# Weight stream of a 256-token model kernel: 1 MB slots and transfers become 512 KB ones, with the ends of the expert layers re-ordered

## The chip, the cores and the metric

The kernel runs on one core of a Trainium2 chip. The metric is the device time of one execution in microseconds (us), lower is better. Three executions of the kernel before took 1793.07, 1799.25 and 1799.32 us, a median of 1799.25. A further execution was profiled.

## The reference, cut to what matters

Everything is float32, 256 tokens of width 1024. A first block of two layers (a convolution and recurrence mixer, an mLSTM mixer, each with a SwiGLU feed-forward of width 2816) is followed by a second block of two layers, and each of these ends in a mixture of experts. The change touches how all weights reach the core, and the code of the mixture:

```
h = modulate(rms_norm(x, g_norm2), shift2, scale2)           # x is 256 x 1024
group  = argmax(h @ w_rg + b_rg)                             # 4 groups
expert = top-2 of the 8 experts of that group (h @ w_re + b_re)
gate   = softmax(group logits)[group] * softmax(top-2 logits)
y = sum over the two experts: gate * (silu(h @ w_gate[e]) * (h @ w_up[e])) @ w_down[e]
x = x + g2 * y
out = rms_norm(x, g_final)                                   # after the second of these layers
```

There are 32 experts of 1024 x 512, 1024 x 512 and 512 x 1024, 6 MB each, and every expert's weights are read in full in both layers: 384 MB of the kernel's 597 MB.

## The kernel before, in words

Weights stream from HBM through slots of 128 x 2048 floats (WT = 2048, 1 MB, rows of 8 KB per partition), all loaded on SyncE's queue (SP). `slot` (L364) hands them out in rotation. The dense weights come through `raw_w` (L389): one 1 MB transfer holds two operands of 128 x 1024, and `split` (L396) divides an operand into a high and a low part on ScalarE (L419) and VectorE (L420). The expert weights come through `load_expert` (L1560, the transfer at L1566): four transfers a matrix and pair of experts, twelve to a pair. `prefetch` fills all free slots ahead of the expert layer, about 20 of them. After that a load waits until TensorE is done with the slot, and it also waits for the landing of the load eight before it, since the framework gives the queue's transfers eight semaphores in turn.

An expert layer (`phase_moe`, L1584) starts with `route` (L1400): transposes of x, router logits, a chain of small VectorE operations that ends in `pos` (the place of every token in its expert's 64 slots) and `W` (its weight). Four matmuls that write an unused bank stand in the middle (NWR, L1432), and the operations for W have a low priority in the order of the queues. Then come 16 pairs of experts, in a fixed order on TensorE (`in_order`). `gather` (L1622) runs for two pairs at a time: eight selection tiles on VectorE (L1626) and four quarters of matmuls, each followed by two evictions into XT (L1637 on ScalarE, L1639 on VectorE). A pair (L1658) is the gate and the up product, silu and a multiply (L1663, L1664), the scatter of the pair before, transposes (L1672, L1681), the down product in two halves of 512 columns, and the split of its result (L1691, L427, L428). In the products the two experts stand side by side in the array, and the trace holds two records to each matmul of the code. `bcast_cols` (L1110) spreads g2 over the partitions with eight small products; it stands in pair 0, between the up product and the transposes.

After pair 5 (PROV) a branch (`overflow`, L1509 to L1558) handles experts with over 64 tokens. It isn't taken here, but its body issues transfers on SP. At the end of a layer `add_x` (L649) adds each token tile to x in two halves and forms the mean square, and after the second layer `final` (L1720) multiplies by the gain and stores four quarters on SP.

Of the kernel before, what the change touches and what calls it, by code (L numbers as in the profile page):

```python
# [16 lines left out]
S = 256  # L17
# [5 lines left out]
WT = 2048  # L23
# [21 lines left out]
NWR = 4  # L45
# [94 lines left out]
def host_layout(inp):  # L140
# [58 lines left out]
    st = np.stack(st).reshape(-1, 2, 128, 1024).transpose(0, 2, 1, 3).reshape(-1, 128, WT)  # L199
    out["wst"] = np.ascontiguousarray(st)  # L200

    a = g["w_ada_2"].reshape(2, 1024, 24, 2, 128).transpose(0, 2, 4, 3, 1)
    out["wada"] = np.ascontiguousarray(a).reshape(48, 128, WT)
# [55 lines left out]
    for n, k in (("w_gate_2", "wg"), ("w_up_2", "wu")):  # L259
        a = g[n].reshape(2, NEXP, 2, 4, 128, 512).transpose(0, 1, 2, 4, 3, 5)  # L260
        out[k] = np.ascontiguousarray(a).reshape(2, NEXP, 2, 128, WT)
    a = g["w_down_2"].reshape(2, NEXP, 4, 128, 2, 512).transpose(0, 1, 4, 3, 2, 5)
    out["wd"] = np.ascontiguousarray(a).reshape(2, NEXP, 2, 128, WT)
# [4 lines left out]
class K:  # L268
    def __init__(self, ctx, first, tc, A, out):
        self.ctx, self.tc, self.A, self.out = ctx, tc, A, out  # L270
        nc = self.nc = tc.nc
        self.slots, self.held, self.sps = [], [], []
        self.n_pool = 0
        self.const = ctx.enter_context(tc.tile_pool(name="const", bufs=1))
        self.sm = ctx.enter_context(tc.tile_pool(name="sm", bufs=4))
        self.taps = {}

        self.spare = ctx.enter_context(tc.tile_pool(name="spare", bufs=SPB))
# [64 lines left out]
    def ring(self, es, n, side=None):  # L343

        self.n_pool += 1
        pool = es.enter_context(self.tc.tile_pool(name=f"ring{self.n_pool}", bufs=n, **({"side": side} if side else {})))
        self.slots = [pool] * n + self.slots
        es.callback(lambda: setattr(self, "slots", [p for p in self.slots if p is not pool]))
# [40 lines left out]
    def raw_w(self):  # L389
        i = self.n_w  # L390
        self.n_w += 1
        if i % 2 == 0:
            self.cur_w = self.slot()
            self.last_w = self.nc.sync.dma_start(self.cur_w, self.A["wst"][i // 2])
        return self.cur_w[:, (i % 2) * 1024:(i % 2) * 1024 + 1024]

    def split(self, w):
# [3 lines left out]
        if sp is self.spare:  # L401
            hl = sp.tile([128, WT], F32R, name="w")
            hi, lo = hl[:, 0:n], hl[:, n:2 * n]
        else:
            hi = sp.tile([128, n], F32R, name="hi")
            lo = sp.tile([128, n], F32R, name="lo")
# [703 lines left out]
def bcast_cols(self, col, dst):  # L1110

    for h in range(2):
        ps = self.ps.tile([128, 512], F32, name="ps")
# [263 lines left out]
def moe_setup(self, l, p):  # L1377
# [12 lines left out]
    wrG = self.kvp.tile([128, 2, D], F32, name="cb")[:, 0].rearrange("p (k e) -> p k e", k=8)  # L1390
# [9 lines left out]
def route(self, raw, tmp, keep):  # L1400
# [15 lines left out]
    for t in range(2):  # L1416
        for h in range(2):
# [4 lines left out]
            if t == 0:  # L1422
                nc.scalar.activation(raw[:, t, 512 * h:512 * h + 512], ps, AF.Copy)
            else:
                nc.vector.tensor_copy(raw[:, t, 512 * h:512 * h + 512], ps)
        pl = self.pa.tile([128, 512], F32, name="pa")
        for k in range(8):
            self.mm(pl[:, 0:RN], raw[:, t, 128 * k:128 * k + 128], wrG[:, k, 0:RN], start=(k == 0), stop=(k == 7))
# [48 lines left out]
    with self.background():  # L1477
# [14 lines left out]
    return rs, pos, W  # L1492
# [16 lines left out]
def overflow(self, l, p, rs, pos, W, fl, acc, w, hid, hT, XT, g2):  # L1509
# [4 lines left out]
    with tc.If(flag):  # L1514
# [4 lines left out]
        for t in range(2):  # L1519
            nc.sync.dma_start(wd[t], wv[:, t])  # L1520
        for t in range(2):
# [6 lines left out]
            with tc.For_i(0, NEXP, 1) as e:  # L1528
                wc = p.tile([128, 1], F32, name="wc", bufs=2)
                nc.sync.dma_start(wc, wd[t, :, ds(e, 1)])  # L1530
                gu = []
                for nm in ("wg", "wu"):
                    ps = self.gu.tile([128, 512], F32, name="gu")
                    for q in range(4):
                        nc.sync.dma_start(w, self.A[nm][l, ds(e, 1), q // 2, :, 1024 * (q % 2):1024 * (q % 2) + 1024].rearrange(
# [11 lines left out]
                for h in range(2):  # L1547
                    py = self.gu.tile([128, 512], F32, name="gu")
                    for q in range(2):
                        nc.sync.dma_start(w, self.A["wd"][l, ds(e, 1), h, :, 1024 * q:1024 * q + 1024].rearrange(  # L1550
# [25 lines left out]
def expert_pair(self, l):  # L1576

    while len(self.ready) < 4:
        self.prefetch(l, 1)
    w, self.ready = self.ready[:4], self.ready[4:]  # L1580
# [3 lines left out]
def phase_moe(self, l):  # L1584
    nc, tc = self.nc, self.tc
    with ExitStack() as es:
# [3 lines left out]
        self.ring(es, n)  # L1590

        late = self.last_slot if l else self.slots[0]
        if l:
            self.prefetch(l, n)
        raw = late.tile([128, WT], F32, name="w").rearrange("p (t d) -> p t d", t=2)
        if not l:
            self.prefetch(l, n - 1)
# [4 lines left out]

        g2 = cst2[:, 0:D]
        hid = p.tile([128, 512], F32, name="hid")
        rs, pos, W = self.route(raw, g2, cst2[:, D:D + 128])
        if l:
            self.slots.insert(0, late)
        self.prefetch(l, 1)
# [13 lines left out]
        def gather(pr):  # L1622

            for t in range(2):
                for e in range(4):
                    nc.vector.tensor_scalar(P[:, t, SLOT * e:SLOT * e + SLOT], iota, pos[:, t, 2 * pr + e:2 * pr + e + 1], rs[t],  # L1626
                                            op0=ALU.is_equal, op1=ALU.mult)
            for q in range(4):
# [12 lines left out]
        def product(x, w, n):  # L1641
# [8 lines left out]
        def scatter(pr):  # L1650

            for t in range(2):
                for h in range(2):
# [4 lines left out]
        def pair(pr):  # L1658
            gu = []
            for m in range(2):  # L1660
                wt = self.expert_pair(l)
                gu.append(product(XT[:, :, 128 * (pr % 2):128 * (pr % 2) + 128], lambda j, k: wt[j][k // 4][:, 512 * (k % 4):512 * (k % 4) + 512], 8))
# [3 lines left out]
            if pr and pr != PROV + 1:  # L1666
# [21 lines left out]
            for h in range(2):  # L1688
                c = slice(512 * h, 512 * h + 512)
                py = product(hT, lambda j, k: wt[j][h][:, 512 * k:512 * k + 512], 4)  # L1690
# [19 lines left out]
        self.xrs, self.early = [None, None], None  # L1710
# [3 lines left out]
        if l == 1:  # L1714
            self.final()
# [3 lines left out]
def final(self):  # L1719
    nc = self.nc  # L1720
    g = self.slot()[:, 0:D]
    i = BROW["g_final"]
    nc.sync.dma_start(g, self.A["brow"][i:i + 1].to_broadcast([128, D]))
    o = self.slot().rearrange("p (t d) -> p t d", t=2)
    for t in range(2):
        for h in range(2):
            c = slice(512 * h, 512 * h + 512)
            nc.vector.scalar_tensor_tensor(o[:, t, c], self.x[:, t, c], self.xrs[t], g[:, c], op0=ALU.mult, op1=ALU.mult)  # L1728
            nc.sync.dma_start(self.out[128 * t:128 * t + 128, c], o[:, t, c])


for _f in (moe_setup, load_expert, prefetch, expert_pair, route, flag, overflow, phase_moe, final):
# [4 lines left out]
def kernel(ctx: ExitStack, tc: tile.TileContext, A, out: bass.AP):  # L1737
    with ExitStack() as right:
        with ExitStack() as first:
# [14 lines left out]
            def early():  # L1754
                k.sps = [p for p in k.sps if p is not k.spare]
                k.held = [k.spare] * SPB
                for _ in range(R2Z):
                    k.hold(right, 1)
                k.last_slot = k.held[-1]
# [3 lines left out]
            def tail():  # L1763
# [4 lines left out]
                k.prefetch(0, R2A, k.held[-R2A:])  # L1768

            k.phase_even(early, tail)  # L1770
            k.prefetch(0, R1)
        k.hold(right, R2B)
        k.prefetch(0, R2B, k.held[-R2B:])
        k.slots = k.held[:-R2B] + k.slots + k.held[-R2B:]
# [4 lines left out]
        k.slots = [p for p in k.slots if p not in (k.spare, k.last_slot)]  # L1779
        k.sps = spare[:]  # L1780
        k.phase_odd(lambda: k.hold(right, R2D))
        k.slots = k.slots[:NPD] + k.held + k.slots[NPD:] + spare
# [21 lines left out]
```

## Time and profile before

| quantity | value |
|---|---|
| three runs | 1793.07, 1799.25, 1799.32 us |
| profiled execution, device time | 1797.08 us |
| its span in the trace | 1795.3 us |
| granted TensorE clock over the span | 0.991 of full |
| TensorE busy | 1717.4 us (96%) |
| VectorE, ScalarE busy | 954.6 us (53%), 593.6 us (33%) |
| moved by DMA | 597.14 MB, mean 333 GB/s |
| SP's hardware queue | 82944 packets, 589.73 MB, 82.0% of 16 engines' span |

Times in the trace run from the start of the span. TensorE's busy time counts matmuls from their issue to a modelled end, so a share of 96% is no statement of how close it is to its peak. The DMA share is the mean busy share of 16 engines, and a little over 1 where packets overlap. The first expert layer lies at about 740 to 1218 us, the second at about 1312 to 1795 us; between them stands the short convolution mixer.

### The profile page before, as it was taken

Reading aid. Unit: us, or ns where it says so; the run is one execution under the profiler, and the core shown is the slowest. Engines: PE = TensorE matmul, PEld = TensorE weight load, DVE = VectorE, ACT = ScalarE, POOL = GpSimd, SP = SyncE. Lnnn points to the kernel's source line nnn. Section 1 sums busy time; section 2 is a strip of 40 time slices with the busy share of each in tenths; the row PEclk is TensorE's granted clock in tenths of the full one; section 3 lists DMA queues with packets and bytes.
Section 4 is the critical chain, followed back from the end, with each engine's and each line's share of the span. In section 5 each row is a group of like instructions: output and inputs, shape, how many; then the busy total and the mean of one; then the engine's idle time right before and its main releaser. Section 6 shows DMA issues by size and latency. Waiting matters only on the chain. (4 is left out here: it accounts for less than half of the span.)

```text
span 1795.3 us, 22692 instructions
## 1 busy us (share of the span) xinstructions
PE 1717.4 (96%) x8858; PEld 1095.2 (61%) x8858; DVE 954.6 (53%) x1960; ACT 593.6 (33%) x1024; POOL 31.1 (2%) x45
## 2 busy tenths in 40 slices
PE   9989999999999999999989999999999999999997
PEld 8878887887888776743444344439964434444442
DVE  8979998887988877522221232227652122221222
ACT  7655545675545556211111111115421011110111
POOL 0000000010000000000000000000000000000000
PEclk9999999999999999999999999999999999999999
DMA  8367786646888763789999999999569999999996
GB/s 303 118 269 276 287 333 236 228 148 241 330 331 324 273 242 146 285 361 420 420 382 419 420 420 420 419 420 373 214 221 420 420 411 391 420 420 420 420 421 283
DMA packets 85059, 597.14 MB, mean 333 GB/s; under 512 B 9808, under 2 KB 10320, under 8 KB 14032
## 3 DMA queue, kind: packets, MB, share of 16 engines
q1 hardware_dynamic: 82944, 589.73, 82.0%
q10 hardware_dynamic: 2000, 5.87, 1.0%
q8 instruction: 72, 1.18, 0.3%
q14 instruction: 43, 0.35, 0.1%
HBM read 594.52 MB, written 1.05 MB: 332 GB/s over the span
## 5 line engine op out<-in xcount | busy, mean ns | idle before, releaser
L431 PE MATMUL gu<-w,XT 128*64 128x512 f32 x2048 | 447.9, 593 | 4.4 <-DMA w<-in_wu_dram 4.1
L431 PEld LDWEIGHTS gu<-w,XT 128*64 128x64 f32 x2048 | 147.2, 137 | 297.0 <-issue 285.0
L431 PE MATMUL gu<-w,kc 128*64 128x512 f32 x1024 | 226.8, 595 | 8.7 <-ACT kc L1673 8.5
L1664 DVE TENSOR_TENSOR hid<-hid,gu 128x512 f32<-128x512 f32 x32 | 22.0, 688 | 382.7 <-PE gu L431 358.6
L420 DVE TENSOR_TENSOR w<-w 128x1024 fp32r<-128x1024 f32 (+1 forms) x157 | 164.2, 1055 | 29.4 <-ACT w L419 29.1
L419 ACT ACTIVATE w<-w 128x1024 fp32r<-128x1024 f32 (+1 forms) x157 | 142.2, 925 | 68.1 <-PE pa L431 17.8
L431 PE MATMUL pq<-xhl,w 128*128 128x256 f32 (+1 forms) x880 | 159.9, 338 | 0.5 <-DVE xhl L595 0.5
L431 PEld LDWEIGHTS gu<-w,kc 128*64 128x64 f32 x1024 | 70.7, 137 | 143.3 <-issue 129.4
L419 ACT ACTIVATE hi<-w 128x1024 fp32r<-128x1024 f32 (+1 forms) x128 | 117.5, 938 | 106.0 <-PE pa L431 45.1
L420 DVE TENSOR_TENSOR lo<-w,hi 128x1024 fp32r<-128x1024 f32 (+1 forms) x128 | 135.6, 1069 | 28.1 <-ACT hi L419 27.2
L431 PEld LDWEIGHTS pq<-xhl,w 128*128 128x128 f32 x880 | 137.0, 189 | 20.9 <-DVE xhl L595 1.1
L431 PE MATMUL ps<-vc,x 128*128 128x256 f32 x512 | 117.5, 388 | 9.1 <-PEq L1514 6.3
L1087 DVE SCALAR_TENSOR_TENSOR wa<-wa,cb 128x1024 f32<-128x1024 f32 x96 | 116.7, 1217 | 4.2 <-DMA wa<-in_wada_dram 4.1
L431 PE MATMUL ps<-xhl,w 128*128 128x256 f32 x960 | 118.0, 284 | 0.5 <-DVE xhl L425 0.3
L427 ACT ACTIVATE cb<-hid 128x512 fp32r<-128x512 f32 x64 | 40.3, 630 | 233.7 <-DVE hid L1691 230.9
L431 PEld LDWEIGHTS ps<-xhl,w 128*128 128x128 f32 x960 | 116.4, 190 | 1.3 <-DVE xhl L425 0.6
L431 PEld LDWEIGHTS ps<-vc,x 128*128 128x128 f32 x512 | 99.2, 195 | 25.3 <-issue 7.1
L1691 DVE SCALAR_TENSOR_TENSOR hid<-gu,ws,cst 128x512 f32<-128x512 f32 x64 | 48.0, 750 | 115.1 <-PE gu L431 110.5
L1637 ACT ACTIVATE XT<-ps,adac,G 128x256 f32<-128x256 f32 x64 | 36.0, 562 | 203.6 <-DVE XT L1639 203.6
L431 PE MATMUL pq<-xhl,hi 128*128 128x512 f32 x264 | 93.7, 397 | 0.0
L1639 DVE TENSOR_SCALAR XT<-ps,G,adac 128x256 f32<-128x256 f32 x64 | 34.7, 542 | 93.1 <-PE ps L431 93.1
L1663 ACT ACTIVATE hid<-gu 128x512 f32<-128x512 f32 x32 | 19.1, 597 | 174.8 <-PE gu L431 174.8
(371 smaller groups left out, 2168.7 us busy)
## 6 DMA issues: line engine op xcount, KB each, us to landing
w<-in_wu_dram SPq DMA_DIRECT2D x128, 1024.0 KB, 19.4
w<-in_wg_dram SPq DMA_DIRECT2D x128, 1024.0 KB, 19.8
w<-in_wd_dram SPq DMA_DIRECT2D x128, 1024.0 KB, 19.8
w<-in_wst_dram SPq DMA_DIRECT2D x126, 1024.0 KB, 5.2
wa<-in_wada_dram SPq DMA_DIRECT2D x44, 1024.0 KB, 7.0
wa<-in_wada_dram SPq DMA_DIRECT2D x8, 512.0 KB, 3.7
brow<-in_brow_dram ACTq DMA_DIRECT2D x7, 512.0 KB, 4.3
x<-in_x_dram SPq DMA_DIRECT2D x2, 512.0 KB, 4.8
```

The costliest lines, as they stand in the source:

```text
L419: self.nc.scalar.activation(hi[:, c], w[:, c], AF.Copy)
L420: self.nc.vector.tensor_sub(lo[:, c], w[:, c], hi[:, c].bitcast(F32))
L427: self.nc.scalar.activation(hi, v, AF.Copy)
L431: self.nc.tensor.matmul(*a, **k)
L1087: nc.vector.scalar_tensor_tensor(junk if j else w, w, 1.0, self.cb[:, j], op0=ALU.mult, op1=ALU.mult, accum_out=d[:, i:i + 1])
L1637: nc.scalar.activation(XT[:, k], o, AF.Identity, scale=G2[:, k:k + 1], bias=sh[:, k:k + 1])
L1639: nc.vector.tensor_scalar(XT[:, k], o, G2[:, k:k + 1], sh[:, k:k + 1], op0=ALU.mult, op1=ALU.add)
L1663: nc.scalar.activation(hid, gu[0], AF.Silu)
L1664: nc.vector.tensor_mul(hid, hid, gu[1])
L1691: nc.vector.scalar_tensor_tensor(hid, py, ws, g2[:, c], op0=ALU.mult, op1=ALU.mult)
```

## The change

All streamed weights come in slots and transfers of 128 x 1024 floats (WT = 1024, 512 KB, rows of 4 KB), with twice as many slots in each pool, so the memory stays the same. `raw_w` loads one operand at a time, from a layout in which each is contiguous. `load_expert` reads one half of each 8 KB row of the same layout as before: eight transfers a matrix and pair, 24 to a pair. High and low parts in the spare pool are two slots. The copy of x for the router no longer takes a slot: it lies in the second half of the tile `cb` and in `kc`.

In `route` the transposes and logits of token tile 0 get the priority of the place where that tile is ready, the four idle matmuls are gone and the g2 products stand in their place, and the operations for W are issued behind the selection tiles of the first gather. Of that gather, quarters 2 and 3 stand inside the first gate product, ahead of k = 2 and k = 4. In the branch's body the transfers are issued by GpSimd. In the last pair the scatter of pair 14 stands between the gate and the up product, and scatters go through the halves of the columns in the outer loop. The end of a layer adds both token tiles for the first half of the columns, then for the second; in the second layer x is multiplied by the final gain on the way, and the stores, after a scaling on ScalarE (tile 0) and VectorE (tile 1), go to SP's and ScalarE's queues.

```diff
-WT = 2048
+WT = 1024
-NWR = 4
@@ raw_w
-        if i % 2 == 0:
-            self.cur_w = self.slot()
-            self.last_w = self.nc.sync.dma_start(self.cur_w, self.A["wst"][i // 2])
-        return self.cur_w[:, (i % 2) * 1024:(i % 2) * 1024 + 1024]
+        w = self.slot()
+        self.last_w = self.nc.sync.dma_start(w, self.A["wst"][i])
+        return w
@@ route
-    pl = self.pa.tile([128, 512], F32, name="pa")
-    for i in range(NWR):
-        self.mm(pl, raw[:, 1, 0:128], raw[:, 0, 0:512], start=(i == 0), stop=(i == NWR - 1))
+    with self.ahead():
+        logits(0)
+    logits(1)
+
+    fill()
...
-    with self.background():
+    def weights():
@@ overflow
-            nc.sync.dma_start(wd[t], wv[:, t])
+            nc.gpsimd.dma_start(wd[t], wv[:, t])
...
@@ load_expert
-    pr, r = divmod(i, 12)
-    m, r = divmod(r, 4)
+    pr, r = divmod(i, 24)
+    m, r = divmod(r, 8)
     e, q = 2 * pr + r % 2, r // 2
     w = self.slot(slots)
-    self.nc.sync.dma_start(w, self.A[("wg", "wu", "wd")[m]][l, e, q])
+    self.nc.sync.dma_start(w, self.A[("wg", "wu", "wd")[m]][l, e, q // 2][:, WT * (q % 2):WT * (q % 2) + WT])
@@ product
             for k in range(n):
+                if k in between:
+                    gather(0, between[k])
@@ scatter
-            for t in range(2):
-                for h in range(2):
+            for h in range(2):
+                for t in range(2):
@@ pair
+                if m and pr == n_pair - 1:
+                    scatter(pr - 1)
...
+                                  {2: [2], 4: [3]} if pr + m == 0 else {}))
...
-            if pr and pr != PROV + 1:
+            if pr and pr not in (PROV + 1, n_pair - 1):
                 scatter(pr - 1)
...
         with self.in_order():
-            gather(0)
-        with self.background():
-            self.bcast_cols(self.adacol(l, "g2"), g2)
+            gather(0, range(2))
+        with tc.issue_after(self.chosen.ins):
+            weights()
@@ end of phase_moe
-        for t in range(2):
-            self.add_x(t, acc[t], junk=[junk[:, 0], junk[:, 1]])
+        for h in range(2):
+            c = slice(512 * h, 512 * h + 512)
+            for t in range(2):
+                x = self.x[:, t, c]
+                nc.vector.tensor_add(x, x, acc[t][h])
+                self.meansq([x, None] if h == 0 else [None, x], sums[t], junk[:, h])
+            if l and h == 0:
+                for t in range(2):
+                    nc.vector.tensor_mul(o[t][:, c], self.x[:, t, c], g[:, c])
+        for t in range(2):
+            self.xrs.append(self.rstd2(sums[t]))
+            if l:
+                nc.vector.tensor_mul(o[t][:, c], self.x[:, t, c], g[:, c])
```

## Rows read from the trace of the kernel before

**Rows 1.** The page: GB/s moved in each of 40 slices of the span.

```profile
GB/s 303 118 269 276 287 333 236 228 148 241 330 331 324 273 242 146 285 361 420 420 382 419 420 420 420 419 420 373 214 221 420 420 411 391 420 420 420 420 421 283
```

**Rows 2.** Windows: stretch, its us, busy (x records) of five engines, PEclk, DMA share, GB/s.

```profile
760.00:770.00 10.00, 10.00 (x48) 5.45 (x48) 3.41 (x11) 3.20 (x5) 0.00 (x0) 1.00 0.21 66
...
1000.00:1100.00 100.00, 97.69 (x456) 44.26 (x452) 23.80 (x56) 12.80 (x22) 0.00 (x0) 1.00 1.01 420
...
1330.00:1340.00 10.00, 10.00 (x43) 6.91 (x43) 4.54 (x15) 3.40 (x5) 0.00 (x0) 0.87 0.03 14
...
1610.00:1770.00 160.00, 152.76 (x702) 63.67 (x704) 37.61 (x85) 18.87 (x33) 0.00 (x0) 1.00 1.01 420
```

**Rows 3.** Timeline, SP: the issues of each layer's last down weights.

```profile
1178.95 7.78 SPq L1566 DMA_DIRECT2D w<-in_wd_dram  x4
...
1751.90 7.81 SPq L1566 DMA_DIRECT2D w<-in_wd_dram  x4
```

**Rows 4.** Landings by line: conditioning loads of 512 KB (L1078), expert weights (L1566).

```profile
DMA to landing us min/median/max: 3.5/3.7/7.0
...
DMA to landing us min/median/max: 4.7/19.8/21.4
```

**Rows 5.** Timeline, TensorE: the last down product of either layer.

```profile
1203.36 7.09 PE L431 MATMUL gu<-w,kc 128*64 128x512 f32 x32 [0.47 <-ACT kc L1673]
...
1776.18 7.09 PE L431 MATMUL gu<-w,kc 128*64 128x512 f32 x32 [0.47 <-ACT kc L1673]
```

**Rows 6.** Waits of TensorE's weight loads from 1600 us on: total, times, longest.

```profile
PEld gu L431 <- DMA w<-in_wu_dram: 7.9, 6, 2.3
...
PEld gu L431 <- DMA w<-in_wg_dram: 1.2, 1, 1.2
```

**Rows 7.** Issue and landing of two early loads on SP, rows of 4.5 KB and 4 KB.

```profile
5.17 0.33 SPq L1157 DMA_DIRECT2D cst<-in_cst_dram  x1
...
5.54 0.44 SPq L1160 DMA_DIRECT2D cb<-in_brow_dram  x1
...
DMA to landing us min/median/max: 10.6/10.6/10.6
...
DMA to landing us min/median/max: 6.4/9.0/11.5
```

**Rows 8.** Windows while x and the first constants land.

```profile
4.00:6.00 2.00, 2.00 (x4) 0.90 (x3) 0.00 (x0) 1.01 (x3) 0.00 (x0) 1.00 1.07 424
```

**Rows 9.** Timeline: the first gate product of either layer, and SP's next load.

```profile
757.48 6.74 PE L431 MATMUL ps<-vc,x 128*128 128x256 f32 x30 [0.19 <-DVE vc L1626]
...
764.15 13.95 PE L431 MATMUL gu<-w,XT 128*64 128x512 f32 x64
...
767.83 4.24 SPq L1566 DMA_DIRECT2D w<-in_wd_dram  x4
...
1328.98 8.43 PE L431 MATMUL ps<-vc,x 128*128 128x256 f32 x30 [0.19 <-DVE vc L1626]
...
1341.02 4.24 SPq L1566 DMA_DIRECT2D w<-in_wd_dram  x4
```

**Rows 10.** The branch: SP's own wait in either layer, then windows behind it.

```profile
SPq L1514 <- SPq L1514: 18.8, 2, 16.3
...
SPq L1514 <- SPq L1514: 19.1, 3, 14.1
...
900.00:920.00 20.00, 19.53 (x94) 7.66 (x92) 3.19 (x10) 1.82 (x3) 0.00 (x0) 1.00 0.83 337
...
1470.00:1490.00 20.00, 19.53 (x94) 7.57 (x92) 3.90 (x8) 2.40 (x4) 0.00 (x0) 1.00 0.83 335
```

**Rows 11.** Timeline: the g2 products in pair 0 of the second layer.

```profile
1351.23 2.05 PE L431 MATMUL ps<-cst,adac 128*128 128x128 f32 x16
```

**Rows 12.** Timeline: the end of the kernel, last scatters and last scaling.

```profile
1785.51 1.44 PE L431 MATMUL pa<-cb,PT 128*128 128x512 f32 x5 [0.23 <-DVE cb L428]
...
1790.76 1.41 DVE L1728 SCALAR_TENSOR_TENSOR w<-x,rs,w 128x512 f32<-128x512 f32 x2 [0.44 <-POOL rs L558]
```

More of the change, by code (lines that the diff above doesn't have):

```diff
@@ L345, in ring @@
         self.n_pool += 1
-        pool = es.enter_context(self.tc.tile_pool(name=f"ring{self.n_pool}", bufs=n, **({"side": side} if side else {})))
-        self.slots = [pool] * n + self.slots
+        pool = es.enter_context(self.tc.tile_pool(name=f"ring{self.n_pool}", bufs=2 * n, **({"side": side} if side else {})))
+        self.slots = [pool] * (2 * n) + self.slots
         es.callback(lambda: setattr(self, "slots", [p for p in self.slots if p is not pool]))
@@ L401, in split @@
         if sp is self.spare:
-            hl = sp.tile([128, WT], F32R, name="w")
-            hi, lo = hl[:, 0:n], hl[:, n:2 * n]
+            hi, lo = (sp.tile([128, WT], F32R, name="w")[:, :n] for _ in range(2))
         else:
@@ L1107, in gain, with bcast_cols @@
     return G
-def bcast_cols(self, col, dst):
+def bcast_cols(self, col, dst, pools=None):
     for h in range(2):
-        ps = self.ps.tile([128, 512], F32, name="ps")
+        ps = pools[h].tile([128, 512], F32, name="pa") if pools else self.bank()
         for k in range(4):
@@ L1389, in moe_setup @@
     nc.sync.dma_start(rb, self.A["brow"][i:i + 1, 64 * l:64 * l + 36].to_broadcast([128, 36]))
-    wrG = self.kvp.tile([128, 2, D], F32, name="cb")[:, 0].rearrange("p (k e) -> p k e", k=8)
+    wrG = self.kvp.tile([128, 2, D], F32, name="cb")
+    self.wrGx = wrG[:, 1]
+    wrG = wrG[:, 0].rearrange("p (k e) -> p k e", k=8)
     nc.gpsimd.memset(wrG, 0.0)
@@ L1491, in route @@
             nc.vector.scalar_tensor_tensor(W[:, t], A0[:, t], w0[:, t:t + 1], W[:, t], op0=ALU.mult, op1=ALU.add)
-    return rs, pos, W
+    return rs, pos, W, weights
 def flag(self, p, pos):
@@ L1590, in phase_moe @@
         self.ring(es, n)
[L1592 to L1597, printed above, removed]
+        self.prefetch(l, 2 * n)
+        raw = [self.wrGx, self.kvp.tile([128, 2, 2 * S], F32, name="kc").rearrange("p a s -> p (a s)")]
         G2, sh = self.router[:2]
@@ L1604, in phase_moe @@
         hid = p.tile([128, 512], F32, name="hid")
[L1605 to L1608, printed above, removed]
+        rs, pos, W, weights = self.route(raw, hid, cst2[:, D:D + 128], lambda: self.bcast_cols(self.adacol(l, "g2"), g2, [self.pa, self.pa]))
         iota = self.cs("iota")[:, 1:65]
@@ L1620, in phase_moe, with gather @@
         n_pair = NEXP // 2
-        def gather(pr):
-            for t in range(2):
[L1625 to L1628, printed above, removed]
+        def gather(pr, qs=range(4)):
+            if 0 in qs:
+                for t in range(2):
+                    for e in range(4):
+                        self.chosen = nc.vector.tensor_scalar(P[:, t, SLOT * e:SLOT * e + SLOT], iota,
+                                                              pos[:, t, 2 * pr + e:2 * pr + e + 1], rs[t],
+                                                              op0=ALU.is_equal, op1=ALU.mult)
+            for q in qs:
                 ps = self.bank()
@@ L1709, in phase_moe @@
                     gather(pr + 1)
-        self.xrs, self.early = [None, None], None
+        self.early = None
         junk = XT.rearrange("p (h k) s -> p h (k s)", h=4)
-        for t in range(2):
-            self.add_x(t, acc[t], junk=[junk[:, 0], junk[:, 1]])
-        if l == 1:
-            self.final()
-    self.tap(f"moe{l}", self.x.rearrange("p t d -> p (t d)"))
-def final(self):
+        sums = [self.sm.tile([128, 2], F32, name="xss") for _ in range(2)]
+        if l:
+            g, o = self.final_gain()
@@ L1720, in final, with final_gain @@
+        self.early = tc.cur_priority
+        if l:
+            self.final(o)
+    self.tap(f"moe{l}", self.x.rearrange("p t d -> p (t d)"))
+def final_gain(self):
+    g = self.slot()
+    i = BROW["g_final"]
+    self.nc.sync.dma_start(g, self.A["brow"][i:i + 1].to_broadcast([128, D]))
+    return g, [self.slot() for _ in range(2)]
+def final(self, o):
     nc = self.nc
-    g = self.slot()[:, 0:D]
-    i = BROW["g_final"]
-    nc.sync.dma_start(g, self.A["brow"][i:i + 1].to_broadcast([128, D]))
@@ L1724, in final @@
-    o = self.slot().rearrange("p (t d) -> p t d", t=2)
     for t in range(2):
         for h in range(2):
[L1727 to L1732, printed above, removed]
+            v = o[t][:, 512 * h:512 * h + 512]
@@ L1733 @@
+            if t == 0:
+                nc.scalar.activation(v, v, AF.Copy, scale=self.xrs[t])
+            else:
+                nc.vector.tensor_scalar(v, v, self.xrs[t], None, op0=ALU.mult)
+            (nc.sync if h == 0 else nc.scalar).dma_start(self.out[128 * t:128 * t + 128, 512 * h:512 * h + 512], v)
+for _f in (moe_setup, load_expert, prefetch, expert_pair, route, flag, overflow, phase_moe, final_gain, final):
     setattr(K, _f.__name__, _f)
```

55 lines of the change are left out of this document (28 added, 27 removed).

## The prediction

> **What bounds the kernel now.** The strip of GB/s comes first [rows 1]: from slice 17 on it stands at 420 but for a dip in slice 20, the mixer between the expert layers (slices 28 and 29) and slice 33. The windows say the same inside the layers, 420 GB/s at a DMA share of 1.01, and show where the stream rests before each: 0.21 busy at 760 to 770 us and 0.03 at 1330 to 1340 [rows 2]. There all slots are full and wait for the first product. Elsewhere TensorE is busy nearly throughout, and before 740 us the stream has room, so what matters lies in the two expert layers.
>
> In each layer TensorE and the stream run a race, and they finish together. SP's four last down loads of the first layer leave over 7.78 us from 1178.95, the last at 1178.95 + 7.78 - 0.33 = 1186.4 [rows 3]; a load lands some 19.9 us after its issue when the queue is full [rows 4], so at 1206.3. TensorE runs that product from 1203.36 to 1210.45 and begins its second half at 1206.9 [rows 5]: 0.6 us of slack. In the second layer the last lands at 1759.4 + 19.9 = 1779.3, and the product ends at 1783.27. There the waits name transfers: weight loads stood idle 9.1 us for wu and wg, seven times, of which 7 x 0.29 is their normal spacing, so 7.1 us [rows 6]. Whatever moves the stream by d moves the second layer by nearly d, and the first by d once its slack is gone.
>
> **The change part by part.** The sum is made against the profiled execution's 1797.1 us, 0.12% under the median of 1799.25.
>
> *Rows of 4 KB in place of 8 KB.* The bytes are the same, the pieces half as long. The saturated stretch is 1206.3 - 767.8 - 3.5 (the branch's gap, below) = 435 us in the first layer and about the same in the second. No stretch of the trace streams 4 KB rows for long. Nearest are two loads at the start: one with 4.5 KB rows issued at 5.17 and landed 10.6 us later, at 15.8, and behind it in the same queue 512 KB with 4 KB rows, issued at 5.54 and landed 11.5 later, at 17.0 [rows 7]. The 1.27 us between them compare with 1.25 for half of 1 MB at 420 GB/s: 2% more, with landings given to 0.1 us. Two readings of a window bound it. At 4 to 6 us, when x lands in 4 KB rows, 424 GB/s flow [rows 8]: no cost, and I count no gain either. But there the share is 1.07, so 396 GB/s for a full share against 416 in the long windows: 5% more engine time. I take 2%, since those two loads are back to back and the window is short. That is +8.7 us per layer for the stream, with 0 and +21.8 as ends. [...]
>
> *Transfers of 512 KB.* Lone loads of 512 KB land in 3.5 us at best and those of 1 MB in 4.7 [rows 4], so the part that doesn't grow with size is 2 x 3.5 - 4.7 = 2.3 us. Eight in flight take 8 x 1.27 = 10 us to move, which covers that. I cost it at nothing; with fewer than three in flight it would show. SP issues one load per 0.33 us of its own time and needs one per 1.25.
>
> *The stream starts again sooner.* Before, gather ends, 16 records of the gate product run (764.15 to 767.6) and the first two slots come free; SP's next load goes at 767.83, and at 1341.02 in the second layer [rows 9]. After, two quarters of gather, then k = 0 and 1: two slots of 512 KB are free after 16 records of gather (3.5 us from 756.6) and 8 of the product (1.8 us), about 762.2. Then each megabyte follows 3.5 us later (a quarter and two k), until the quarters are done. By 771.5 the new order has had 3 MB moved, the old one 3.7 us x 0.42 = 1.5. The rest, 1.5 MB, is -3.8 us for the stream in each layer.
>
> *The branch.* SP waits 18.8 and 19.1 us there [rows 10], while the loads in flight drain; behind it the share is 0.83 over 20 us in both layers, against 1.01 elsewhere. 0.18 of 20 us is 3.6, lost bytes (337 against 420 GB/s) say 4.0; I take a gap of 3.5 us in either layer, near the smaller. With the transfers on GpSimd SP has nothing in the body and shouldn't stop; GpSimd does, and nothing of it is due before the layer's end. -3.5 for the stream in each layer.
>
> *Router and g2.* Four low-priority operations (about 0.15 us each) leave VectorE's chain: -0.5 to TensorE. The idle matmuls lie beside that chain and cost nothing now. The g2 products take 2.05 us in pair 0 [rows 11], of which the wait for the multiply would take 1.0 anyway: -1.0. In the second layer ScalarE's table load for exp may now fall among the gather's evictions, 0 to 1.3 us. Router tile 0 ahead of the last output matmuls: as much lost there as won later, 0. TensorE rests more before gather; at 1330 to 1340 the granted clock is already 0.87, and 30 records took 8.43 us in place of 6.74, so up to 1.7 us [rows 2, 9]. I take 0, with both for the range.
>
> *Ends of the layers.* After the stream's last piece only 8 records are left, 8/32 x 7.09 = 1.8 us [rows 5]; now it is 3.5, and in the second layer 4.0. In the last pair the scatter no longer hides the multiply behind the up product: +1.0 on TensorE, nothing where the stream is late. From the last scatters to the last scaling it takes 1785.51 to 1792.17, 6.7 us [rows 12]. The new chain has two scatters, an add, a square, the sums, a power and two scalings behind the last product: about 5 us, so -1.5. I take the same in the first layer.
>
> *Before 740 us* the loads are twice as many and as long in sum; slots filled ahead hide them, and TensorE's dense work covers SP's extra issues. 0; with that cover gone each wait would cost up to 1.25 us, a transfer. The final gain's load stays behind the last weights, and the stores on two queues are in the end's -1.5.
>
> *Sum.* First layer: the last weight lands at 1206.3 + 8.7 - 3.8 - 3.5 = 1207.7, its product could end at 1209.5. TensorE by itself would end it at 1210.45 - 0.5 - 1.0 + 1.0 = 1209.95: TensorE decides, by a little. With the end, -2.0. The mixer between the layers is TensorE's and keeps its length. Second layer: 1779.3 - 2.0 + 8.7 - 3.8 - 3.5 = 1778.7, the product ends at 1780.5, 2.8 before 1783.27; with the end -4.3. 1797.1 - 4.3 = 1792.8, written 1793. Where the stream decides both layers, the whole is 2d - 22.1 us for a cost d per layer: break-even at d = 11.05 (2.5%).
>
> **The rivals.** *Rows of 4 KB cost nothing.* For it speaks the 424 GB/s window [rows 8]. Then TensorE decides both layers: the second product ends at 1783.3 less the 7.1 of waits, less 2.0, 0.5 and 1.0, plus 1.0, so 1773.7; that is 9.6 sooner, and with the end -11.1: 1786. *Short rows are dear,* the rival on the other side: per-row and per-transfer work in the 16 engines at the 5% that the busy share suggests [rows 8]. With d = 21.8 it is 2 x 21.8 - 22.1 = +21.5, 1819. It makes the kernel slower than before above 2.5%, and passes +9 at d = 15.5, 3.6%. [...] *SP stops at the branch all the same,* because it takes the branch with every engine. The queue then drains as before, half as long but with half the bytes, and 7.0 us come back, less the 0.4 by which TensorE decided: 1799. Against it: the wait in the trace is one for transfers of the body.
>
> **How the numbers follow.** Forecast 0.45 (its own range 1787 to 1800), free rows 0.30, dear rows 0.16, the branch 0.09. A measurement of this kernel tells 0.5% (9 us) from no change: under 1790 is faster, over 1808 slower. Faster takes the free rows (0.28) and the better part of the forecast's spread (0.09): 0.37. Slower takes most of the dear rows (0.13) and small parts of the forecast and the branch (0.04): 0.17. Same 0.46. The range leaves out the far end of the free rows and the upper half of the dear ones: 1780 to 1809.
>
> **What would show it.** Windows inside the layers: about 412 GB/s if I am right, 420 for free rows, under 405 for dear ones. No dip behind the branch and no wait of SP there, or the third rival holds. The first load after the rest goes 5 us sooner after the start of gather than now. In the second layer TensorE's waits name transfers in the last pairs, more than the 7.1 us of now for rows over 2.5%, none for free rows; the last product ends under 2 us behind the last landing. Wrong altogether would be a TensorE that waits for transfers already in the middle of the first layer, or a phase before 740 us that is longer by over 3 us.

## The result and the profile after

The changed kernel takes 1812.55 us (median of five runs, 1811.21 to 1816.57) against 1798.02 of the kernel before (1793.07 to 1799.32): a ratio of 1.0089, 95% interval 1.0073 to 1.0105. Forecast was 1793, range 1780 to 1809, with 0.17 on slower by over 0.5%. The profiled execution took 1811.44 us with a span of 1809.6. Against the 1795.3 of before the 14.3 us lie here (ends of records from the timelines; the norm is GpSimd's power):

| stage | before | after | change | forecast |
|---|---|---|---|---|
| start to the norm ahead of the first expert layer | 744.6 | 752.2 | +7.6 | 0 |
| that norm to the end of the layer's last down product | 465.8 | 470.1 | +4.3 | -0.5 |
| from there to the next norm | 6.2 | 5.3 | -0.9 | -1.5 |
| that norm to the first gather of the second layer | 111.4 | 110.7 | -0.7 | 0 |
| that gather to the end of the last down product | 455.2 | 458.4 | +3.2 | -0.8 |
| from there to the end of the span | 12.0 | 12.9 | +0.9 | -1.5 |

The stages make up the whole span, so that they sum to the difference says nothing of the causes.

The changed kernel's page: GB/s over 40 slices (before: [rows 1]), and the landing of an expert load (before: [rows 4]).

```profile
GB/s 312 140 240 284 280 321 236 221 141 232 332 326 323 280 220 165 270 349 409 409 408 409 409 409 409 409 409 406 228 242 404 408 409 408 409 409 409 409 409 289
...
w<-in_wd_dram SPq DMA_DIRECT2D x256, 512.0 KB, 10.2
```

Its windows, columns as in [rows 2]: the long ones, those behind the branch [rows 10], and the first 15 us after the restart.

```profile
1000.00:1100.00 100.00, 98.38 (x459) 40.91 (x456) 23.20 (x50) 11.36 (x19) 0.00 (x0) 1.00 1.03 409
1610.00:1770.00 160.00, 155.37 (x702) 68.73 (x701) 40.73 (x93) 20.56 (x35) 0.00 (x0) 1.00 1.03 409
...
900.00:920.00 20.00, 20.00 (x94) 6.72 (x96) 3.91 (x9) 1.86 (x3) 0.00 (x0) 1.00 1.03 409
1470.00:1490.00 20.00, 19.53 (x94) 7.66 (x92) 5.22 (x11) 2.45 (x4) 0.00 (x0) 1.00 1.03 409
...
770.00:785.00 15.00, 15.00 (x70) 6.43 (x68) 2.87 (x10) 3.01 (x4) 0.00 (x0) 1.00 0.76 250
1345.00:1360.00 15.00, 15.00 (x68) 6.43 (x68) 3.03 (x11) 3.01 (x4) 0.00 (x0) 1.00 0.82 261
```

The layers stream at 409 GB/s in place of 420. The dip behind the branch is gone, but a new one stands behind the restart, where the share is 0.76 and 0.82.

Its timelines, TensorE (first gather, last down products, as [rows 9] and [rows 5]) and SP (first load after the rest, last loads), then TensorE's waits for transfers from 1600 us on [rows 6].

```profile
762.83 0.70 PE L427 MATMUL ps<-vc,x 128*128 128x256 f32 x2 [1.17 <-DVE vc L1621]
763.72 4.98 PE L427 MATMUL ps<-vc,x 128*128 128x256 f32 x14 [0.20 <-DVE vc L1621]
...
1214.25 8.03 PE L427 MATMUL gu<-w,kc 128*64 128x512 f32 x32 [0.47 <-ACT kc L1674]
...
1788.66 8.02 PE L427 MATMUL gu<-w,kc 128*64 128x512 f32 x32 [0.47 <-ACT kc L1674]
```

```profile
770.59 10.10 SPq L1568 DMA_DIRECT2D w<-in_wd_dram  x8
...
1201.19 9.29 SPq L1568 DMA_DIRECT2D w<-in_wd_dram  x8
...
1345.34 10.54 SPq L1568 DMA_DIRECT2D w<-in_wd_dram  x8
...
1775.63 9.25 SPq L1568 DMA_DIRECT2D w<-in_wd_dram  x8
```

```profile
PEld gu L427 <- DMA w<-in_wg_dram: 8.7, 17, 1.1
PEld gu L427 <- DMA w<-in_wu_dram: 7.3, 13, 1.1
...
PEld gu L427 <- DMA w<-in_wd_dram: 2.7, 8, 0.7
```

Both last down products take 8.0 us in place of 7.09: the stream now paces the end of both layers. The waits are 18.7 us in 38, less 38 x 0.29 of normal spacing 7.7 us (272 gaps of the same loads with nothing to wait for are 76.8 us, 0.28 each). The last loads land at 1201.19 + 9.29 - 0.33 + 10.2 = 1220.4 and 1794.8.

Ahead of the expert layers the norms show where the time goes. GpSimd's power of the norm behind each of the two dense feed-forwards, before and then after:

```profile
300.32 0.93 POOL L558 TENSOR_TENSOR rs<-ms,mhalf 128x1 f32<-128x1 f32 x1 [184.98 <-DVE ms L556]
...
619.21 0.93 POOL L558 TENSOR_TENSOR rs<-ms,mhalf 128x1 f32<-128x1 f32 x1 [183.94 <-DVE nsink L1204]
```

```profile
303.21 0.86 POOL L554 TENSOR_TENSOR rs<-ms,mhalf 128x1 f32<-128x1 f32 x1 [187.43 <-DVE ms L552]
...
625.97 0.55 POOL L554 TENSOR_TENSOR rs<-ms,mhalf 128x1 f32<-128x1 f32 x1 [186.05 <-DVE adac L1090]
```

Counted from the norm at 105.8 us (106.0 after), the first feed-forward takes 2.8 us more, the mixer up to the norm at 430.0 us (433.3 after) 0.4 more, the second feed-forward 3.5 more, and what follows 0.8. VectorE's waits for conditioning weights (the loads of `in_wada`, from which the scales and shifts of the norms are made) up to 744 us (total, times, longest), before and then after:

```profile
DVE wa L1087 <- DMA wa<-in_wada_dram: 4.1, 3, 2.2
```

```profile
DVE wa L1083 <- DMA wa<-in_wada_dram: 12.0, 13, 1.6
```

And these waits of the changed kernel in the two feed-forwards alone, 106 to 300 us and 430 to 620 us, where the kernel before had none and 0.8 us:

```profile
DVE wa L1083 <- DMA wa<-in_wada_dram: 5.2, 4, 1.6
...
DVE wa L1083 <- DMA wa<-in_wada_dram: 3.9, 6, 1.5
```

TensorE's timeline where the first feed-forward ends, before and then after:

```profile
305.07 0.41 PE L614 MATMUL pn<-cst,xn 128*128 128x128 f32 x2 [1.52 <-DVE xn L611]
...
306.66 1.42 PE L431 MATMUL ps<-w,xhl 128*128 128x512 f32 x5 [0.53 <-ACT xhl L594]
```

```profile
308.40 0.66 PE L610 MATMUL pn<-cst,xn 128*128 128x128 f32 x2 [3.47 <-DVE xn L607]
...
310.00 2.48 PE L427 MATMUL ps<-w,xhl 128*128 128x512 f32 x5
```

TensorE rests 3.47 us there in place of 1.52, and the next five matmuls take 2.48 us in place of 1.42: the clock has fallen (granted 0.50 over 310 to 312.5 us). The granted clock over 300 to 350 us is 0.90 after, 1.00 before. But the stretch from 300 to 430 us is only 0.4 us longer as a whole, so this fall carries little of the 7.6 us.

### The profile page after: what moved, and what is told of

Read it like the earlier page. It is cut to its first block, busy times and chain, and to the rows that moved or that the text cites. A ratio compares the mean times of both kernels' runs of the same rounds, so it can differ in the third digit from the quotient of the medians.

```text
span 1809.6 us, 23828 instructions
## 1 busy us (share of the span) xinstructions
PE 1723.8 (95%) x8842; PEld 1097.7 (61%) x8842; DVE 957.0 (53%) x1962; ACT 595.2 (33%) x1026; POOL 32.1 (2%) x45
## 5 line engine op out<-in xcount | busy, mean ns | idle before, releaser
L427 PE MATMUL gu<-w,XT 128*64 128x512 f32 x2048 | 456.2, 594 | 1.7 <-DMA w<-in_wg_dram 0.8
L415 ACT ACTIVATE hi<-w 128x1024 fp32r<-128x1024 f32 (+1 forms) x128 | 117.7, 937 | 102.9 <-PE pa L427 37.9
L1083 DVE SCALAR_TENSOR_TENSOR wa<-wa,cb 128x1024 f32<-128x1024 f32 x96 | 116.3, 1220 | 12.1 <-DMA wa<-in_wada_dram 12.0
L1674 ACT ACTIVATE kc<-ps 128x512 f32<-128x512 f32 x32 | 19.1, 597 | 185.3 <-PE ps L1673 185.3
## 6 DMA issues: line engine op xcount, KB each, us to landing
w<-in_wu_dram SPq DMA_DIRECT2D x256, 512.0 KB, 10.2
w<-in_wg_dram SPq DMA_DIRECT2D x256, 512.0 KB, 10.2
w<-in_wd_dram SPq DMA_DIRECT2D x256, 512.0 KB, 10.2
```

The lines of the kernel that those rows point to most:

```text
L415: self.nc.scalar.activation(hi[:, c], w[:, c], AF.Copy)
L427: self.nc.tensor.matmul(*a, **k)
L1083: nc.vector.scalar_tensor_tensor(junk if j else w, w, 1.0, self.cb[:, j], op0=ALU.mult, op1=ALU.mult, accum_out=d[:, i:i + 1])
L1674: nc.scalar.activation(hT, pt.rearrange("p (k s) -> p k s", k=4), AF.Copy)
```

## The experiments

Times are medians; ratios are to the kernel before, timed beside.

**1. What the parts do alone.** `e1_reorder_1mb` keeps 1 MB slots and all re-orderings, `e2_512k_alone` the 512 KB pieces and the old order.

```diff
 e1: -WT = 1024
     +WT = 2048      # raw_w, load_expert, pools as before; all else as in the change
 e2: -WT = 2048
     +WT = 1024      # raw_w, load_expert, pools as in the change; route, gather, branch, ends as before
```

> The re-orderings alone: slots and transfers of 1 MB as before, everything else as in the changed kernel. Theory S (all of the loss comes with the 512 KB pieces): the stream stays at 420 GB/s in the expert layers, the norm ahead of the first expert layer is done at 744.6 us as before (752.2 in the changed kernel), no dip behind the branch, TensorE's 7 us of waits for transfers in the second layer are gone, about 1788 us. Rival R (the re-orderings disturb the order of the dense phase, and the half clock in the first gather costs as much as the branch gives): the norm comes at 750 us or later, about 1797 us or more.

> The 512 KB slots and transfers alone, with the order of before (idle matmuls, gather in one piece, branch's transfers on SP, old ends); the copy of x for the router lies where the changed kernel has it. Theory S: 409 GB/s, the norm ahead of the first expert layer at about 752 us, per layer 12 us more for the stream with nothing won back at the branch or the restart, so 1797 + 7.6 + 10 + 12, about 1826 us. Rival R: the norm at 745 us, about 1818 us or less.

`e1` 1794.99 us, ratio 0.9997 (0.9985 to 1.0009); `e2` 1826.39 us, 1.0171 (1.0147 to 1.0196). The norm, from GpSimd's timeline of `e1`, then `e2`:

```profile
744.90 0.86 POOL L557 TENSOR_TENSOR rs<-ms,mhalf 128x1 f32<-128x1 f32 x1 [82.95 <-DVE ms L555]
```

```profile
752.99 0.86 POOL L555 TENSOR_TENSOR rs<-ms,mhalf 128x1 f32<-128x1 f32 x1 [84.85 <-DVE ms L553]
```

All of the loss comes with the 512 KB pieces, in both stages. The re-orderings are worth 1826.4 - 1812.6 = 13.8 us where the stream is late, but nothing clear of noise at 1 MB (the interval of `e1` holds 1): there the stream runs at 420 GB/s without a dip behind the branch, TensorE's waits for transfers from 1600 us on are down from 9.1 to 1.8 us, and TensorE decides. I had expected 1788 for `e1` and missed by 7: I had given the first layer a gain that TensorE didn't allow. From the norm to the end of its last down product `e1` takes 467.0 us in place of 465.8 in the first layer, and from gather 450.0 in place of 455.2 in the second.

**2. Length of a row or size of a transfer.**

```diff
 e3: -dma_start(w, A[...][l, e, q])                      # 128 rows of 8 KB
     +dma_start(w.rearrange("p (h f) -> p h f", h=2), A[...][l, e, q].rearrange("h p f -> p h f"))
 e4: +for s in (0:64, 64:128):
     +    dma_start(w[s], A[...][l, e, q][s])            # 64 rows of 8 KB each
```

> As e1_reorder_1mb, but each expert transfer of 1 MB is made of rows of 4 KB (the two halves of a slot come from two blocks of DRAM). If the length of a row sets the rate: 409 GB/s in the layers and 8 to 16 us above e1_reorder_1mb. If the size of a transfer (its fixed part, the queue's turn) sets it: 420 GB/s and the time of e1_reorder_1mb.

> As e1_reorder_1mb, but each expert slot is filled by two transfers of 512 KB with rows of 8 KB, 64 partitions each. If the length of a row sets the rate: 420 GB/s and the time of e1_reorder_1mb within 2 us. If the size of a transfer sets it: 409 GB/s or less, 8 to 16 us above it.

`e3` 1809.67 us, 1.0079 (1.0055 to 1.0103), 14.7 above `e1`; `e4` 2430.85 us (2350.88 to 2453.64). Windows of `e1`, `e3` and `e4`:

```profile
1000.00:1100.00 100.00, 97.69 (x457) 44.29 (x454) 23.61 (x56) 12.62 (x22) 0.00 (x0) 1.00 1.01 420
```

```profile
1000.00:1100.00 100.00, 98.28 (x460) 44.32 (x454) 22.86 (x53) 11.87 (x21) 0.00 (x0) 1.00 1.02 409
```

```profile
1000.00:1100.00 100.00, 66.75 (x233) 27.37 (x233) 14.39 (x34) 7.05 (x12) 0.00 (x0) 0.84 1.02 228
```

Transfers of 1 MB with rows of 4 KB run at the same 409 GB/s as those of 512 KB. In the layers the row's length sets the rate (`e1` to `e3`, 420 to 409 GB/s), and at rows of 4 KB the size of a transfer costs nothing with eight in flight (the changed kernel's 10.2 us to landing at 409 GB/s are 4.2 MB, eight of 512 KB). `e4` didn't answer its question: by writing half the partitions it changed something larger, 228 GB/s in place of 420.

**3. Branch and first gather**, in the changed kernel.

```diff
 e5: -nc.gpsimd.dma_start(...)       # all four in the branch's body
     +nc.sync.dma_start(...)
 e6: -gather(0, range(2))
     +gather(0)
     -{2: [2], 4: [3]} if pr + m == 0 else {}
     +{}
```

> The changed kernel with the transfers of the branch's body issued on SP again, as before. If the step on the branch was right, SP waits there for its eight loads to land, 512 KB each, the share of DMA behind it falls below 1.03, and both layers, where the stream ends last, get about 3.5 us longer: 1819 us. Rival: with 512 KB loads the queue drains and refills in half the time, so only 2 us per layer come back: 1816 us. If the branch never held the stream: 1812 us.

> The changed kernel with the first gather in one piece ahead of the gate product. As the prediction had it (the quarters between win 3.8 us for the stream in each layer): about 1820 us. By what the trace of the changed kernel shows (loads go 3.5 to 5 us sooner after the start of gather, but one slot per two k, so the stream runs at half rate for the next 15 us): 0.7 to 2.3 us per layer, about 1815 us. Rival, the quarters win nothing at all: 1812 us.

`e5` 1825.84 us, 1.0157 (1.0137 to 1.0178); `e6` 1819.33 us, 1.0123 (1.0104 to 1.0143). Both executions that were profiled also lost 4 us before the first layer, though VectorE's and ScalarE's order there is that of the changed kernel (norm at 756.4 and 756.6; VectorE waited 16.1 and 14.7 us for conditioning weights, 12.0 in the changed kernel), so the totals may overstate. From gather to the end of the last down product the layers take 464.5 and 464.8 us in `e5`, 460.2 and 460.9 in `e6`, against 459.5 and 458.4. The branch on SP thus costs 5.0 and 6.4 us with pieces of 512 KB, more than the 3.5 expected, though SP waits only half as long there as with 1 MB (18.7 us in place of 37.9); the quarters win 0.8 and 2.5. SP's waits at the branch in both layers of `e5` (total, times, longest), and the windows behind it:

```profile
SPq L1516 <- SPq L1516: 18.7, 5, 9.3
```

```profile
910.00:930.00 20.00, 19.53 (x94) 7.66 (x92) 3.78 (x9) 1.82 (x3) 0.00 (x0) 1.00 0.83 305
1490.00:1510.00 20.00, 19.53 (x94) 7.65 (x92) 4.45 (x10) 1.86 (x4) 0.00 (x0) 1.00 0.80 293
```

**4. The dense phase**, on `e1` (`e14`: on the changed kernel).

```diff
 e7:  -dma_start(cur_w, A["wst"][i // 2])
      +for h in range(2): dma_start(cur_w[:, 1024 * h:][:, :1024], A["wst"][i // 2][:, 1024 * h:][:, :1024])
 e9:  -dma_start(cur_w, A["wst"][i // 2])      # wst laid out by operand
      +dma_start(cur_w.rearrange("p (h f) -> p h f", h=2), A["wst"][i // 2].rearrange("h p f -> p h f"))
 e10: e7, and e13: e1, and e14: the changed kernel, with
      -nc.sync.dma_start(w, A["wada"][i]...)
      +nc.gpsimd.dma_start(w, A["wada"][i]...)
```

> As e1_reorder_1mb, but each 1 MB slot of the dense phase is filled by two transfers of 512 KB (rows of 4 KB); slots, high and low parts and the expert loads stay at 1 MB. Theory T (the 7.6 us ahead of the expert layers come from the smaller transfers: twice as many turns and landings in the queue, conditioning weights late behind them): the norm ahead of the first expert layer at about 752 us, 1802 us in all. Theory G (they come from the slots of 512 KB, which change when and in which order ScalarE and VectorE split the weights, so that TensorE rests at the ends of the blocks and its clock falls): the norm at 745 us, 1795 us in all.

> As e1_reorder_1mb, but each 1 MB transfer of the dense phase is made of rows of 4 KB; the order of the instructions on TensorE, VectorE and ScalarE is the same as there. If the loss ahead of the expert layers comes from short rows, as in the expert layers: the norm at 752 to 754 us, 1803 us in all. If it comes from the number of transfers and the order that is planned around them: the norm at 745 us, 1795 us in all, and short rows cost only where the stream is saturated.

> As e7_dense_2x512 (norm at 754.2 us), but the 44 conditioning loads of 1 MB are issued on GpSimd's queue and no longer stand behind twice as many weight loads on SP's. If the late conditioning loads (VectorE waited 9.6 us for them, 2.3 in e1_reorder_1mb) carry the loss of the dense phase: the norm at 745 to 747 us, 1795 us in all. If they are a symptom: still 752 us or more, 1802 us.

> The control of e10_cond_on_pool: e1_reorder_1mb (1 MB transfers, norm at 744.9 us) with the 44 conditioning loads on GpSimd's queue. If smaller transfers make the conditioning loads late, nothing is late here and nothing is won: norm at 744 to 746 us, 1795 us. If the move is worth 6 us to any version: norm at 739 us, 1790 us.

> The changed kernel with the 44 conditioning loads on GpSimd's queue. If their lateness carries most of the loss of the dense phase: norm at 745 to 748 us in place of 752.2, 1806 us in all. If not: 752 us or later, 1812 us.

| kernel | us | ratio (interval) | norm at | VectorE's waits for conditioning |
|---|---|---|---|---|
| `e7`, two transfers a slot | 1803.38 | 1.0035 (1.0020 to 1.0049) | 754.2 | 9.6 us |
| `e9`, 4 KB rows alone | 1794.19 | 0.9983 (0.9974 to 0.9993) | 747.7 | 3.2 us |
| `e10`, `e7` with conditioning on GpSimd | 1798.58 | 1.0014 (1.0002 to 1.0025) | 748.3 | 2.6 us |
| `e13`, control with 1 MB | 1795.38 | 1.0003 (0.9991 to 1.0016) | 743.8 | 3.7 us |
| `e14`, the change with it | 1809.29 | 1.0090 (1.0074 to 1.0107) | 746.8 | 3.4 us |

The norm of `e7` and of `e10`:

```profile
754.21 0.86 POOL L559 TENSOR_TENSOR rs<-ms,mhalf 128x1 f32<-128x1 f32 x1 [84.01 <-DVE ms L557]
```

```profile
748.27 0.86 POOL L559 TENSOR_TENSOR rs<-ms,mhalf 128x1 f32<-128x1 f32 x1 [84.21 <-DVE ms L557]
```

The number of transfers costs the dense phase 9.3 us even where slots stay at 1 MB (theory T, G falls). Short rows alone (`e9`) show 2.8 in the one execution that was profiled and nothing in the median time. Taking the conditioning loads off SP's queue brings the norm forward by 5.9 us (`e7` to `e10`) and 5.4 (the change to `e14`), and by about 1 at 1 MB (`e13`), where kernels of one order spread from 743.5 to 745.6. The times follow in part: `e10` is 4.8 us below `e7`, but `e14`, expected at 1806, has the ratio of the changed kernel (1.0090 against 1.0089), and its profiled span is shorter by 3.7 us, since it takes 1.7 longer behind that norm.

So most of the loss goes with conditioning weights that come late. They are slower on their way by 1.3 us at most: such a load of 1 MB lands 7.0 us after its issue in the kernel before, 7.5 in the changed one, 8.3 in `e7` and, on GpSimd's queue, 8.0 in `e10` (medians). They are issued late. On SP they stand in one order with the weight loads, and in the first feed-forward of the changed kernel SP stood 139 us until VectorE's splits freed a slot, and never for a landing.

What isn't separated is the order of the work. With other transfers the build arranges VectorE's and ScalarE's order anew: of VectorE's 1962 instructions some 90 stand elsewhere in `e7` than in `e1`. It does so too when the conditioning loads change their queue (some 120 from `e7` to `e10`, 110 from the change to `e14`, 70 from `e1` to `e13`). `e13` shows that a new order by itself need cost nothing; no version with small transfers and the old order was tried. `e14` stays 14 us above `e13`; 3 of them lie ahead of the layers, the rest is the stream's part.

**5. The clock in the first gather, and the end.**

```diff
 e8:  e1, behind fill():
      +for i in range(2): mm(pl[:, 0:448], raw[1][:, 0:128], raw[0][:, 0:448], ...)
 e11: e8, all four scalings on VectorE and stores on nc.sync
 e12: e8, second layer: add_x(t, acc[t]) and final() as before, scatters by token tile
```

> As e1_reorder_1mb, with two idle matmuls (448 columns) behind the g2 products, where TensorE rests 1.65 us ahead of the position products. Theory K (the shorter filling, 1.95 us of g2 products in place of 3.6 us of idle matmuls, let the clock fall in the first gather): the clock is 1.00 at 755 to 765 us, the first 16 records of gather take 3.5 us in place of 5.5, the first layer ends 2 us sooner, and the whole is 1793 us or a little less. Rival: the rest of 1.17 us behind the position products is enough for the fall, nothing changes, 1795 us.

> As e8_idle_back, but all four scalings at the end on VectorE and all four stores on SP, as in the kernel before; the rest of the new end stays. If ScalarE's slower scalings and its queue's stores are what cancelled the shorter end: from the last down product's end to the end of the span 11.4 us in place of 12.7, 1792 us in all. If the time goes in the new order of the adds: 12.7 us, 1793.4.

> As e8_idle_back, but the second layer ends as in the kernel before: adds, norm, scaling and two stores of token tile 0, then of tile 1 (scatters by tile too). If the new end loses because both tiles come out at once and four stores of 256 KB then queue up (share 0.99 over 2 us in the changed kernel, 0.71 at most before): from the last down product's end to the end of the span 12.0 us in place of 12.7, 1792.7 us in all. Rival: the old end is no shorter behind this order, 12.7 us, 1793.4.

`e8` 1793.40 us, 0.9986 (0.9975 to 0.9997); `e11` 1793.00 us, 0.9986 (0.9976 to 0.9996); `e12` 1792.72 us, 0.9978 (0.9968 to 0.9989). TensorE's first gather in `e8`, then `e11`, where the order is the same:

```profile
754.14 0.70 PE L430 MATMUL ps<-vc,x 128*128 128x256 f32 x2 [1.17 <-DVE vc L1627]
755.03 4.81 PE L430 MATMUL ps<-vc,x 128*128 128x256 f32 x14 [0.19 <-DVE vc L1627]
```

```profile
756.16 0.70 PE L430 MATMUL ps<-vc,x 128*128 128x256 f32 x2 [1.18 <-DVE vc L1627]
757.06 3.29 PE L430 MATMUL ps<-vc,x 128*128 128x256 f32 x14 [0.19 <-DVE vc L1627]
```

Theory K falls: with the rest filled the clock still fell in `e8` and `e12` and held in `e11` (granted over 755 to 760 us: 0.69 in `e8`, 1.00 in `e11`; in `e12` the first 16 records took 5.65 us). `e2`, which has the old filling, fell too: 16 records of its first gather take 5.9 us, against 4.2 in the kernel before. The rest of 1.17 us behind the position products stays, and behind it the clock fell in one profiled execution and not in another. That `e8` came out at the 1793 of theory K is not due to it, and its interval overlaps that of `e1`.

At the end, from the last down product: `e8` 12.7 us, `e11` 12.5, `e12` 12.1. Windows over the last stores of the changed kernel, then of the kernel before:

```profile
1803.00:1805.00 2.00, 0.00 (x0) 0.00 (x0) 0.99 (x3) 1.33 (x2) 0.91 (x2) 0.50 0.00 0
1805.00:1807.00 2.00, 0.00 (x0) 0.00 (x0) 0.00 (x0) 0.00 (x0) 0.00 (x0) 0.50 0.99 374
```

```profile
1789.00:1791.00 2.00, 0.00 (x0) 0.00 (x0) 1.56 (x4) 0.00 (x0) 0.92 (x1) 0.75 0.29 112
1791.00:1793.00 2.00, 0.00 (x0) 0.00 (x0) 1.18 (x2) 0.00 (x0) 0.00 (x0) 0.50 0.71 268
```

Adding by halves makes both token tiles ready at once, and 1 MB of stores then moves with nothing left to hide it. Before, tile 0's half was on its way while tile 1 was scaled. ScalarE's scalings and queue were worth 0.2 us at most (`e11`); taking back the whole end by tiles was worth 0.6 (`e12`). Single profiles bear this out: the three kernels with the old end take 12.0 to 12.2 us from there (`e2` is the third), the others with the new one 12.5 to 13.0. `e12` has the lowest time, 4 us under the kernel before and 20 under the change, though its interval overlaps those of `e8`, `e9` and `e11`.

## Why the prediction was wrong, step by step

- **Bound.** Right: the two expert layers are a race of TensorE and the stream, and with the change the stream decides both. It let the dense phase count as covered, which was wrong.
- **Rows of 4 KB.** Mechanism right, size off: I took 2% and 8.7 us per layer; 409 against 420 GB/s is 2.7%, 435 x (420/409 - 1) = 11.7 us, and `e3` shows that it is the row. Two lone loads 1.27 us apart were too short a sample, and the second of them sends one 4 KB row of DRAM to all partitions (L1160 is a broadcast), so it was no stream of such rows at all. The other reading's 396 GB/s for a full share came back (409 at 1.03 is 397), but the share rose with it, from 1.01, and the loss was 2.7% and not 5%. By the measured 11.7 us the sum is +1.3 in place of -4.3.
- **Transfers of 512 KB at nothing.** Right in the layers, where eight are in flight: `e3` has the change's 409 GB/s at 1 MB. In the dense phase the 512 KB pieces did cost time, most likely for another reason (next point).
- **Before 740 us at nothing.** The step that failed by most, 7.6 us. I named full slots and TensorE's dense work as cover and a wait of 1.25 us as the price. That the number of transfers costs this phase so much is shown (`e7`, 9.3 us). Which way it takes is in part argued: what came late were not the streamed weights but the conditioning weights between them on the same queue (4.1 to 12.0 us of VectorE's waits, most of the growth in the two feed-forwards that grew). VectorE has no time to spare there, busy 49.7 of 50 us at 150 to 200 us in the kernel before, so the norms come later. Whether the build's new order takes a part of it stays open.
- **Restart.** -3.8 per layer was forecast; `e6` measures -0.8 and -2.5. Loads do go sooner, 7.8 and 7.1 us after the start of gather in place of 11.2 and 12.9 (11.2 and 10.9 in `e6`), but not after the 5.6 us that I counted. The first two quarters took 5.9 us in place of my 3.5: at the full clock it is 4.2 (first layer of the kernel before), so 0.7 of that was my misreading and 1.7 the half clock (granted 0.66 over 764 to 769 us). I had seen that fall in the second layer, bounded it at 1.7 us, and taken 0. `e6` has it too, so it is no part of what the quarters win. That is little because slots come free one per expert and two k, with quarters of gather between, and the stream runs at a share of 0.76 and 0.82 in place of 1.03 for 15 us, which gives back 3.9 and 3.1 us by the share.
- **Branch.** Right: no wait of SP, no dip. With small pieces it is even worth 5.0 and 6.4 us (`e5`).
- **Router and g2, mixer.** Small, but not as forecast (-0.5 ahead of either layer): norm to first gather went from 12.0 to 10.6 us ahead of the first, and from 12.6 to 13.5 ahead of the second. `e2`, with the old order of the router, has 10.7 and 12.5, so the gain is not the re-ordering's and the loss is. The -1.0 for the g2 products in pair 0 was not measured alone.
- **Ends.** Of -1.5 twice, -0.9 in the first layer; in the second +0.9, since the chain that I counted ended at the scalings and the stores behind it had lost their cover: to the last scaling it is 0.8 us shorter (8.1 in place of 8.9), from there to the end of the span 1.7 longer (4.8 in place of 3.1).
- **Rivals.** *Dear rows* was nearest in time, but 1819 was put at 5% on the rate, and the rate is 2.7%. *Free rows* and *SP stops at the branch* are excluded by the windows. What came true was the line that would prove it wrong altogether: a phase before 740 us longer by over 3 us. It had no rival of its own and no part in the range. The other such line did not come true (no weight load of TensorE's waited more than 0.3 us for a transfer between 800 and 1150 us), and the milder signs came: no dip, a first load 3.5 and 5.9 us sooner, waits of 7.7 us, a last product that ends 1.9 us behind the last landing.

In the prediction's own terms the misses are 7.6 us before 740 us, 5.6 for the rows, 4.3 for the restart and 3.0 for the ends. Together that is more than the 18.6 us between the forecast -4.3 and the measured +14.3, since the branch gave more than was counted and the terms overlap.

## What to carry to other kernels

Smaller pieces of a stream had two prices here. The saturated stretch paid for the length of a row (409 GB/s at 4 KB, 420 at 8 KB) and, at rows of 4 KB, nothing for the size of a transfer (409 at 512 KB and at 1 MB); the stretch that was not saturated paid for their number (9.3 us, `e7`), most likely through other loads on the same queue, so ask which loads lie between the ones that are doubled, and who waits for them. Where two parties finish together, relieving one of them gains only the other's slack: re-orderings worth 14 us beside a slow stream were worth nothing clear of noise beside a fast one. The output that was finished all at once had no cover for its stores (4.8 us from the last scaling to the end, in place of 3.1).

## What the hardware showed that was not expected

- Transfers that fill 64 of 128 partitions, two in turn, moved 228 GB/s at a share of 1.02, against 420 for transfers of all 128 partitions (`e4`). That is at 1000 to 1100 us; at 1610 to 1770 us it was 218 GB/s and at 2000 to 2100 us 247, at the same share. No run shows the cause.
- The clock fell behind the same rest of 1.17 us in one profiled execution (14 records of gather in 4.81 us, `e8`) and not in another with the same code up to there (3.29, `e11`).
- Kernels with the same order of VectorE's and ScalarE's work and 512 KB pieces reached the first expert layer at 752.2 (the change), 753.0 (`e2`), 756.4 (`e5`) and 756.6 us (`e6`); those with 1 MB pieces and rows of 8 KB there at 743.5 to 745.6.
- At the branch that is not taken TensorE stood 6.0 us in the first layer and 0.3 in the second of the kernel before, 6.2 and 0.3 in `e1`. It is the longest stop in the first layer, no version touched it, and no run shows its cause.
